# Store sizes by stage in a masked softmax: a half and two quarters for ten batches, then halves, then whole tiles

## Chip, cores, metric

One core of one Trainium2 chip. The metric is device time in microseconds (us), the median of several executions. The granted clock was 1.0 in every run.

## The reference

For each of 16 batches the softmax runs over the first `lengths[b]` of 256 columns, and the rest is zero:

```python
x: (16, 8, 256, 256) float32;  lengths: 16 integers in [128, 256)
result = zeros_like(x)
for b in range(16):
    m = x[b, :, :, :lengths[b]]
    m = exp(m - max(m, axis=-1))
    result[b, :, :, :lengths[b]] = m / sum(m, axis=-1)
```

A batch is 2.097 MB: 128 partitions x 16 rows x 256 columns. In memory one partition's 16 rows are 16 KB in one piece, for the load as for the store.

## The kernel before

Twelve batch slots lie in on-chip memory. SyncE issues the first four loads and all stores; GpSimd issues the other twelve loads, cut to a width that covers the length. VectorE masks (`min` with a cap), ScalarE takes exp and row sums, VectorE multiplies by the inverse, one half batch at a time.

```python
slots, ahead, half = 12, 4, nt // 2          # nt = 16 rows per partition
parts = [slice(0, half), slice(half, half + half // 2), slice(half + half // 2, nt)]
early = batch - slots
s_st = [sem(f"s_st{b}") for b in range(early)] + [sem("s_st")] * slots
...
load(nc.sync, 0, seq_k)                      # and 1, 2, 3
for b in range(batch):                       # SyncE: the stores
    for k, s in enumerate(parts):
        if k < 2:
            nc.sync.wait_ge(s_out, 2 * b + k + 1)
        nc.sync.dma_start(
            out=out_f[b, :, s, :], in_=xt[:, b % slots, s, :]
        ).then_inc(s_st[b], 16)
nc.sync.wait_ge(s_st[-1], 16 * len(parts) * slots)
...
for n in range(ahead, batch):                # GpSimd: the loads
    if n < slots:
        nc.gpsimd.wait_ge(s_fill, n - ahead + 1)
    else:
        nc.gpsimd.wait_ge(s_st[n - slots], 16 * len(parts))
    pick(length(POOL, n), n, widths + [seq_k])   # one load, width by length
...
# VectorE, per batch: mask(b + 1), then for each half: wait for exp, reciprocal, multiply, s_out + 1
```

The softmax here doesn't subtract the row's maximum and nothing guards it: scores larger than these inputs give would overflow.

Of the kernel before, what the change touches and what calls it, by code (L numbers as in the profile page):

```python
# [21 lines left out]
def kernel(  # L22
# [6 lines left out]
    nc = tc.nc  # L29
    P = nc.NUM_PARTITIONS  # L30

    batch, heads, seq_q, seq_k = x.shape
    rows = heads * seq_q
    assert rows % P == 0
    nt = rows // P
    half = nt // 2
# [4 lines left out]
    slots = min(12, batch)  # L41
# [2 lines left out]
    widths = list(range(160, 248, 8))  # L44
    low = widths[0]

    parts = [slice(0, half), slice(half, half + half // 2), slice(half + half // 2, nt)]
    mid = seq_k // 2

    pool = ctx.enter_context(tc.tile_pool(name="all", bufs=1))  # L50
# [14 lines left out]
    inv_sum = pool.tile([P, batch, nt], F32, name="inv_sum")  # L65
    warm = pool.tile([P, 1], F32, name="warm")

    with tc.tile_critical(no_gpsimd_drain=True):  # L68
        sem = lambda n: ctx.enter_context(nc.semaphore(n))
        s_word = sem("s_word")  # L70
        s_word_p = sem("s_word_p")
        s_ones = sem("s_ones")
# [4 lines left out]
        early = batch - slots  # L77
        s_st = [sem(f"s_st{b}") for b in range(early)] + [sem("s_st")] * slots
# [5 lines left out]
        s_out = sem("s_out")  # L84

        def length(engine, b):

            return nc.values_load(  # L88
                (word_p if engine == POOL else word)[0:1, 2 * b : 2 * b + 1],
                engines=[engine],  # L90
                skip_runtime_bounds_check_because="compared with constants, never an address",
            )
# [9 lines left out]
        for b in range(1, ahead):  # L102
            load(nc.sync, b, seq_k)
        for b in range(batch):
            for k, s in enumerate(parts):
                if k < 2:
                    nc.sync.wait_ge(s_out, 2 * b + k + 1)
                nc.sync.dma_start(
                    out=out_f[b, :, s, :], in_=xt[:, b % slots, s, :]
                ).then_inc(s_st[b], 16)  # L110
        nc.sync.wait_ge(s_st[-1], 16 * len(parts) * slots)



        def pick(v, b, ws):

            if len(ws) == 1:
                load(nc.gpsimd, b, ws[0])
                return
            m = (len(ws) - 1) // 2  # L120
            with nc.gpsimd.If(v <= ws[m]):  # L121
                pick(v, b, ws[: m + 1])
            with nc.gpsimd.Else():  # L123
                pick(v, b, ws[m + 1 :])
# [11 lines left out]
        for n in range(ahead, batch):  # L136
            if n < slots:
                nc.gpsimd.wait_ge(s_fill, n - ahead + 1)
            else:
                nc.gpsimd.wait_ge(s_st[n - slots], 16 * len(parts))  # L140
            pick(length(POOL, n), n, widths + [seq_k])


# [56 lines left out]
        for b in range(batch):  # L200
# [3 lines left out]
            for h in range(2):  # L204
                s = slice(h * half, (h + 1) * half)
# [25 lines left out]
                    if (j + 1) % half == 0:  # L231
                        ins.then_inc(s_exp, 1)


# [1 line left out]
_INS = ['x', 'lengths']  # L236
_OUTS = [((16, 8, 256, 256), 'float32')]
# [25 lines left out]
```

## Time and profile before

| | before |
|---|---|
| time, median of 3 (lowest to highest) | 158.04 us (157.88 to 158.11) |
| profiled span | 155.8 us |
| VectorE, ScalarE busy | 78%, 68% |
| bytes moved, mean rate | 62.11 MB, 399 GB/s |
| last load's data, last store's data | 122.6 us, 153.65 us |

The last row is from the trace's packet records. After the last load the DMA engines do nothing for 31 us but push out stores, and for the last 17 of those no engine but the DMA engines works.

### The profile page before, as it was taken

The page shows a single profiled execution, that of the slowest core. Times are in us where ns is not written, and L with a number is a line of the kernel's source. Part 1 is how long each engine was busy: PE and PEld are TensorE (multiplying, and loading weights), DVE is VectorE, ACT ScalarE, POOL GpSimd, SP SyncE. Part 2 cuts the span into 40 slices and gives each one's busy share as a digit, 9 for nine tenths or more (in the row PEclk, how much of TensorE's full clock was granted, in tenths as well). Part 3 has the DMA queues.
Part 4 walks back from the last instruction along what each step waited for, and adds up shares of the span by engine and source line. Part 5 has one row for each costly group of instructions (what it writes and reads, how often), then busy time and mean ns, then how long its engine had stood idle before and what let it go on. Part 6 is the DMA issues. An engine that isn't in the chain of part 4 may idle for free.

```text
span 155.8 us, 1177 instructions
## 1 busy us (share of the span) xinstructions
PE 0.2 (0%) x1; PEld 0.1 (0%) x1; DVE 120.8 (78%) x99; ACT 105.3 (68%) x514; POOL 25.0 (16%) x27
## 2 busy tenths in 40 slices
PE   0000000000000000000000000000000000000000
PEld 0000000000000000000000000000000000000000
DVE  2566999999999999869995999997968999900000
ACT  3009999997979797929696597978692989200000
POOL 5995045742002002010000000000000000000000
DMA  5999999999999999999999999999999999999991
GB/s 126 421 446 421 437 357 386 411 444 426 378 401 405 414 418 412 419 408 405 422 408 414 407 415 408 407 417 409 422 438 426 409 428 413 424 427 428 425 411 50
DMA packets 11607, 62.11 MB, mean 399 GB/s; under 512 B 1058, under 2 KB 1154, under 8 KB 8786
## 3 DMA queue, kind: packets, MB, share of 16 engines
q1 hardware_dynamic: 7488, 41.95, 65.8%
q0 software_dynamic: 4112, 20.12, 32.1%
q14 instruction: 5, 0.04, 0.1%
q10 hardware_dynamic: 2, 0.00, 0.0%
HBM read 28.51 MB, written 33.55 MB: 398 GB/s over the span
## 4 chain that ended last, share of the span: by engine, by line
DMA 33%; DVE 29%; issue 12%; POOL 6%; another core or an unknown queue 4%; POOLq 2%; SPq 1%; DVEq 0%
DMA xt<-in_x_dram 33%; DVE xt L209 17%; DVE xt L182 10%; POOL xt L133 4%; POOL xt L96 2%; DVE inv_sum L207 1%; DVE cap L167 1%; POOLq L88 1%; POOLq L121 1%; SPq L96 1%; DVEq L195 0%; POOLq L123 0%; DVEq L194 0%; SPq L258 0%
## 5 line engine op out<-in xcount | busy, mean ns | idle before, releaser
L225 ACT ACTIVATE xt<-xt x256 | 102.4, 402 | 26.6 <-DVE xt L182 26.6
L209 DVE TENSOR_TENSOR xt<-xt,inv_sum 128x2048 f32<-128x2048 f32 x32 | 73.3, 2292 | 1.1
L225 ACT ACTIVATION_READ_ACCUMULATOR xt<-xt x256 | 48.0, 187 | 0.0
L182 DVE TENSOR_TENSOR xt<-xt,cap 128x2048 f32<-128x2048 f32 x16 | 36.6, 2287 | 11.5 <-DMA xt<-in_x_dram 11.4
L96 POOL DMA_DIRECT2D xt<-in_x_dram x12 | 12.7, 1056 | 41.6 <-issue 41.5
L133 POOL MEMSET xt<- 128x1536 f32 x8 | 11.0, 1426 | 0.3 <-DVE iota_h L157 0.3
L167 DVE TENSOR_SCALAR cap<-iota_h,len_s 128x256 f32<-128x256 f32 x16 | 8.5, 537 | 0.0
L207 DVE RECIPROCAL inv_sum<-row_sum 128x8 f32<-128x8 f32 x32 | 6.2, 195 | 0.0
L157 DVE TENSOR_SCALAR iota_h<-iota_i 128x256 f32<-128x256 int32 x1 | 0.3, 295 | 2.6 <-POOL iota_i L127 2.6
L218 ACT ACT_TABLE_LOAD x1 | 1.3, 1283 | 1.5 <-SPq L68 1.5
L126 POOL DMA_DIRECT2D word_p<-in_lengths_dram x1 | 0.6, 633 | 1.1 <-SPq L68 1.1
L161 DVE COPY len_s<-len_f 128x16 f32<-128x16 f32 x1 | 0.2, 175 | 0.4 <-PE len_f L146 0.4
L127 POOL IOTA iota_i<- 128x256 int32 x1 | 0.4, 360 | 0.1
L218 ACT ACTIVATE warm<-const-float32-0.0 128x1 f32<-128x1 f32 x1 | 0.2, 203 | 0.0
L130 POOL MEMSET ones<- 1x128 bf16 x1 | 0.2, 194 | 0.0
L146 PE MATMUL len_f<-len_b,ones 1*128 1x16 bf16 x1 | 0.2, 168 | 3.1 <-DVE len_b L159 3.1
L159 DVE CAST len_b<-word 1x16 bf16<-1x16 int32 x1 | 0.2, 155 | 0.0
L247 POOL MEMSET const-float32-0.0<- 128x1 f32 x1 | 0.1, 98 | 0.2 <-issue 0.2
L146 PEld LDWEIGHTS len_f<-len_b,ones 1*128 1x128 bf16 x1 | 0.1, 98 | 3.1 <-POOL ones L130 3.1
L247 POOL MEMSET const-bfloat16-1.0<- 128x1 bf16 x1 | 0.1, 99 | 0.0
L247 POOL MEMSET const-uint8-127<- 128x1 uint8 x1 | 0.1, 99 | 0.0
L247 POOL MEMSET const-float32-1.0<- 128x1 f32 x1 | 0.1, 98 | 0.0
## 6 DMA issues: line engine op xcount, KB each, us to landing
out_dram<-xt SPq DMA_DIRECT2D x16, 1024.0 KB, 22.8
out_dram<-xt SPq DMA_DIRECT2D x32, 512.0 KB, 22.7
xt<-in_x_dram SPq DMA_DIRECT2D x4, 2048.0 KB, 14.4
xt<-in_x_dram POOLq DMA_DIRECT2D x3, 1728.0 KB, 54.0
xt<-in_x_dram POOLq DMA_DIRECT2D x2, 2048.0 KB, 37.6
xt<-in_x_dram POOLq DMA_DIRECT2D x2, 1600.0 KB, 36.3
xt<-in_x_dram POOLq DMA_DIRECT2D x2, 1280.0 KB, 61.5
xt<-in_x_dram POOLq DMA_DIRECT2D x1, 1792.0 KB, 39.9
```

Source lines behind the costliest of these rows:

```text
L88: return nc.values_load((word_p if engine == POOL else word)[0:1, 2 * b : 2 * b + 1], engines=[engine], skip_runtime_bounds_check_because= ...
L96: engine.dma_start(out=xt[:, b % slots, :, :w], in_=x_f[b, :, :, :w]).then_inc(s_ld[b], 16)
L121: with nc.gpsimd.If(v <= ws[m]):
L126: nc.gpsimd.dma_start(out=word64_p, in_=lengths[None, :]).then_inc(s_word_p, 16)
L127: nc.gpsimd.iota(iota_i, pattern=[[1, seq_k]], base=0, channel_multiplier=0).then_inc(s_iota, 1)
L133: nc.gpsimd.memset(xt[:, b, :, low:], 0.0).then_inc(s_fill, 1)
L167: nc.vector.tensor_scalar(out=cap[:, b % 4, :], in0=iota_h, scalar1=len_s[:, b : b + 1], scalar2=-1.0e30, op0=ALU.subtract, op1=ALU.mult,)
L182: return nc.vector.tensor_tensor(out=t[:, :, lo:hi], in0=t[:, :, lo:hi], in1=cap[:, b % 4, None, lo:hi].to_broadcast([P, nt, hi - lo]), op ...
L207: step(nc.vector.reciprocal(out=inv_sum[:, b, s], in_=row_sum[:, b, s]))
L209: ins = nc.vector.tensor_tensor(out=t[:, s, :], in0=t[:, s, :], in1=inv_sum[:, b, s, None].to_broadcast([P, half, seq_k]), op=ALU.mult,)
L218: nc.scalar.activation(out=warm, in_=nc.const_aps.tensor(0.0, (P, 1), F32), func=EXP)
L225: ins = nc.scalar.activation(out=e, in_=e, func=EXP, accum_out=row_sum[:, bass.ds(i, 1), j],)
```

## The change

Its intent: while loads run beside the stores, keep store packets small, so that the loads get their share; once no load is left, make them large, since fewer packets cost less.

```diff
-    parts = [slice(0, half), slice(half, half + half // 2), slice(half + half // 2, nt)]
+    quarter = nt // 4
+    cuts = lambda b: (
+        [0, half, half + quarter, nt]
+        if b < slots - 2
+        else [0, half, nt]
+        if b < slots or b == batch - 1
+        else [0, nt]
+    )
+    def parts(b):
+        return [slice(i, j) for i, j in zip(cuts(b), cuts(b)[1:])]
...
-            for k, s in enumerate(parts):
-                if k < 2:
-                    nc.sync.wait_ge(s_out, 2 * b + k + 1)
+            for s in parts(b):
+                nc.sync.wait_ge(s_out, 2 * b + (s.stop - 1) // half + 1)
...
-        nc.sync.wait_ge(s_st[-1], 16 * len(parts) * slots)
+        nc.sync.wait_ge(s_st[-1], 16 * sum(len(parts(b)) for b in range(early, batch)))
...
-                nc.gpsimd.wait_ge(s_st[n - slots], 16 * len(parts))
+                nc.gpsimd.wait_ge(s_st[n - slots], 16 * len(parts(n - slots)))
```

The diff is cut here: it also moves the line that defines `sem`, which changes nothing on the chip. So batches 0 to 9 stay as they were, 10, 11 and 15 go out in halves (8 KB per partition), 12 to 14 whole (16 KB).

More of the change, by code (lines that the diff above doesn't have):

```diff
@@ L66 @@
     warm = pool.tile([P, 1], F32, name="warm")
+    sem = lambda n: ctx.enter_context(nc.semaphore(n))
     with tc.tile_critical(no_gpsimd_drain=True):
-        sem = lambda n: ctx.enter_context(nc.semaphore(n))
         s_word = sem("s_word")
```

## The prediction

> **What bounds the kernel now.** I read the page first, for what is busy when. The page's second part shows it:
>
> ```profile
> DVE  2566999999999999869995999997968999900000
> ACT  3009999997979797929696597978692989200000
> ...
> DMA  5999999999999999999999999999999999999991
> ```
>
> The DMA row stands at 9 from the second slice to the last but one. VectorE and ScalarE stop five slices (some 19 us) before the end. So the 16 DMA engines bound the kernel, and the end is a drain of stores with nothing else running. The page's chain of waits is no guide here: it stops at VectorE's last multiply (134.10 + 2.29 = 136.4 us), because the trace ties no instruction to the final stores.
>
> Next I cut the span into stages, to see how full the engines are in each (columns: stretch, length, busy time of PE, PEld, DVE, ACT and POOL, clock, DMA share, GB/s):
>
> ```profile
> 45.00:75.00 30.00, 0.00 (x0) 0.00 (x0) 27.51 (x24) 24.28 (x120) 2.85 (x3) 1.00 1.02 413
> 75.00:100.00 25.00, 0.00 (x0) 0.00 (x0) 22.54 (x20) 20.02 (x101) 0.00 (x0) 1.00 1.02 410
> 100.00:123.00 23.00, 0.00 (x0) 0.00 (x0) 19.96 (x17) 17.46 (x87) 0.00 (x0) 1.00 1.02 420
> 123.00:129.30 6.30, 0.00 (x0) 0.00 (x0) 6.23 (x6) 5.72 (x30) 0.00 (x0) 1.00 1.01 421
> 129.30:151.40 22.10, 0.00 (x0) 0.00 (x0) 7.03 (x5) 4.06 (x21) 0.00 (x0) 1.00 1.02 423
> 151.40:154.10 2.70, 0.00 (x0) 0.00 (x0) 0.00 (x0) 0.00 (x0) 0.00 (x0) 1.00 0.36 147
> ```
>
> The share is 1.02, not 1.00: packet records overlap a little, so a packet's recorded length is more than it costs. Only the last 2.7 us are ragged; there the engines finish one after another.
>
> Then one batch of the drain (exactly one period, found by trying edges), from the view of the DMA queues:
>
> ```profile
> DMA packets 432, 2.10 MB, mean 424 GB/s; under 512 B 48, under 2 KB 48, under 8 KB 304
> ...
> q1 hardware_dynamic: 432, 2.10, 101.9%
> ...
> out_dram<-xt SPq DMA_DIRECT2D x1, 1024.0 KB, 17.1
> out_dram<-xt SPq DMA_DIRECT2D x2, 512.0 KB, 16.6
> ```
>
> One batch makes 432 packets: 128 of 8 KB (the half, one per partition), 256 of 4 KB (two quarters), 48 of semaphore updates (3 stores x 16 engines). It takes 4.95 us, and a store lands about 17 us after its issue: that is the backlog in the queue.
>
> **What the Trainium skill says.** All three places are in "DMA: Bandwidth & Descriptors". Section "Where 436 GB/s comes from" gives a ceiling of 435.2 GB/s for the 16 engines. The drain's 424 is 97% of it: the trace agrees, and little is left to gain. Section "Why small descriptors are slow (HBM only)" names a fixed overhead of about 3 cycles per packet, besides descriptor metadata. In the packet records of one engine (the one that ends last but one, followed from packet to packet), 4 KB packets are 159 ns long but start every 155.3 ns (152.326, 152.481, 152.636 us), and 8 KB packets are 309 ns long and start every 305.9 ns (148.275, 148.581, 148.887 us). A straight line through the two pitches gives 150.6 ns per 4 KB, which is 27.2 GB/s per engine or 435 for 16, and 4.7 ns fixed per packet. So the trace shows such an overhead, and gives its size. Section "Queues, rings and completion order" says that each engine takes turns between its queues packet by packet. This explains the change's intent: small store packets beside the loads, large ones when no load is left. No view of this one trace tests it.
>
> **The change part by part.** Stores of batches 0 to 9 keep their sizes, and so do all loads, arithmetic and slots. The third store of these batches gets a wait of its own, on a count that the second store has already waited for: nothing on the path. Loads reuse only the slots of batches 0 to 3, whose three stores and count of 48 are unchanged.
>
> What changes is batches 10 to 15. When do their packets run? Stores of one queue go in order. The last load lands at 123.1 us; batch 9's last quarter lands at 124.3 and batch 10's first half, which is 8 KB in both kernels, at 126.4. Everything that differs therefore runs after the loads, in the pure drain. Up to there I expect the same times, to the noise.
>
> In the drain each engine moves 8 partitions of each store. Per batch and engine:
> - Before: 8 x 305.9 + 16 x 155.3 + 3 semaphore packets. Where one of these lies between two 4 KB packets, their starts are 161 ns apart instead of 155, so it costs about 6 ns. Sum: 2,447 + 2,485 + 18 = 4,950 ns, the 4.95 us measured.
> - Halves (batches 10, 11, 15): eight pairs of 4 KB become eight of 8 KB: 8 x (2 x 155.3 - 305.9) = 38 ns, and one semaphore packet fewer: 44 ns saved.
> - Whole tiles (batches 12, 13, 14): a 16 KB packet should cost 305.9 + 2 x 150.6 = 607 ns by the line. 8 x (305.9 + 310.6 - 607) = 75 ns, and two semaphore packets fewer: 87 ns saved.
>
> Sum: 3 x 44 + 3 x 87 = 393 ns. It is all on the path, since the engines have no gap in the drain. SyncE issues 9 stores fewer (48 to 39), at 0.33 us each when not held up; that lies beside a 17 us backlog and is worth nothing. So 158.04 - 0.39 = 157.65 us.
>
> **The rivals.**
> 1. *Record lengths are the cost.* With mean lengths of 161, 313 (median 309) and, from the 16 KB loads, 611 ns, a half saves 8 x (322 - 311) + 9 = 97 ns and a whole tile 8 x (311 + 322 - 611) + 18 = 194 ns, in all 0.87 us: 157.2. Against it: the share of 1.02, and a cap. After batch 10's first half there are 5.5 batches x 2.097 MB = 11.5 MB left, which take 5.5 x 4.95 = 27.2 us now and 26.5 at 435 GB/s. Not more than 0.7 us can come from packet sizes here.
> 2. *16 KB stores are no better than two of 8 KB.* The 16 KB loads at the start are 611 ns long, and the second and third land 4.89 and 4.91 us after the one before, which is a pitch of 611, not 607. Whether that belongs to loads or to 16 KB is open. For stores it would make the whole tiles save 8 x (616.5 - 611) + 12 = 56 ns and the sum 0.30 us: 157.74.
> 3. *Larger stores start too late.* A whole tile has to wait for the second half's multiply. For batch 14 that ends at 129.22 + 2.29 = 131.5 us; the queue gets to it when batch 13 has landed, at 144.2: 12.7 us to spare. For batch 12 it is 115.1 against 134.3. In the changed kernel the drain is at most some tenths earlier, so no gap can open. If I misread it and the queue ran dry before one tile, one half's multiply, 2.4 us with its reciprocal, would be lost: 160.
> 4. *The issuer is held up.* One store issue took 5.7 us (the longest in the trace), some others 1 to 3: SyncE waits when about ten stores are outstanding. A limit in stores would be relieved by fewer, larger ones; a limit in bytes would stay. Neither matters while the backlog is 17 us.
> 5. *The ragged end.* The last two engines finish at 153.57 and 153.65, the others between 152.0 and 152.84. A lag from earlier stages stays as it is when all engines have the same packets to move; larger last packets could move the end by a few hundredths.
>
> **Range and chances.** I take the middle of the first sum, 157.65. The runs of before spread over 0.23 us (157.88 to 158.11), about half of the gain itself, so I give 157.3 to 158.0. A gain of 2% would be 3.2 us, over four times the cap of 0.7 us: 1%. A loss of 2% needs a dry queue or a loss of pace with 16 KB stores that the loads don't show: 1%.
>
> **What would show it.** In the queue view: 1,296 packets fewer on queue 1 (3 x 144 + 3 x 288, so 6,192), and issues of 16 x 1024, 20 x 512 and 3 x 2048 KB. Loads landing at the same times to some tenths, the last near 123. In a drain stretch of whole tiles 431 GB/s (2.097 MB in 4.863 us), of halves 427, of before 424. The span 0.3 to 0.5 us shorter. I am wrong if the GB/s of the whole-tile stretch stays at 424 or falls, if a gap shows in the DMA row after 126 us, or if the times before 123 us move by more than the drain.

## More of the kernel before

One more view of this kernel, which the prediction did not use and should have: the DMA queues between 60 and 90 us (queue, kind: packets, MB, share of 16 engines). Queue 1 holds SyncE's stores, queue 0 GpSimd's loads.

```profile
q1 hardware_dynamic: 1389, 6.63, 54.3%
q0 software_dynamic: 1389, 5.73, 47.7%
```

The packet counts are equal to the last one. This suggests that, while both queues are full, each gets every other packet, and that the sizes of the packets decide how the bandwidth is shared. Experiments 5 and 6 test it.

## The result

| | before | after |
|---|---|---|
| time, median of 6 (lowest to highest) | 157.96 us (157.84 to 158.11) | 157.68 us (157.54 to 157.99) |
| ratio, 95% interval | | 0.9986 (0.9973 to 0.9998) |

Ratios here are the mean time of one kernel's runs over that of the other's of the same rounds, so not quite the ratio of the medians. The means are 0.23 us apart, 0.14%: a little faster in the interval.

The profile after, the page's busy tenths and packets:

```profile
DVE  2567999999999998949995999997977999910000
ACT  3009999997979695957978397979592989400000
...
DMA  4999999999999999999999999999999999999990
...
DMA packets 10311, 62.11 MB, mean 399 GB/s; under 512 B 914, under 2 KB 1010, under 8 KB 7106
...
q1 hardware_dynamic: 6192, 41.95, 65.4%
```

1,296 packets fewer, all on queue 1, as counted in advance. The DMA row has no gap.

The stages of the drain, same columns as in the prediction:

```profile
100.00:123.00 23.00, 0.00 (x0) 0.00 (x0) 20.08 (x19) 17.57 (x87) 0.00 (x0) 1.00 1.02 420
123.00:129.30 6.30, 0.00 (x0) 0.00 (x0) 6.26 (x4) 5.71 (x29) 0.00 (x0) 1.00 1.01 428
129.30:151.40 22.10, 0.00 (x0) 0.00 (x0) 7.60 (x7) 4.67 (x24) 0.00 (x0) 1.00 1.01 429
151.40:154.10 2.70, 0.00 (x0) 0.00 (x0) 0.00 (x0) 0.00 (x0) 0.00 (x0) 1.00 0.17 70
```

Before 123 us the rate is the same, 420. In the drain it is 429 instead of 423, and in the last, ragged stretch the engines are busy 17% of the time instead of 36%: most of them end earlier.

Two whole tiles of that drain (134.5 to 144.22 us), in the view of the DMA queues:

```profile
DMA packets 288, 4.19 MB, mean 432 GB/s; under 512 B 32, under 2 KB 32, under 8 KB 32
...
q1 hardware_dynamic: 288, 4.19, 100.8%
```

256 packets of 16 KB and 32 semaphore updates take 9.72 us, so 4.86 us per tile. Before, a batch took 4.95. The edges of this stretch were chosen to hold exactly two tiles. A stretch with other edges, also of whole tiles alone, reads less:

```profile
134.50:147.00 12.50, 0.00 (x0) 0.00 (x0) 2.47 (x3) 0.00 (x0) 0.00 (x0) 1.00 1.00 427
```

The view counts a packet where it starts, and sixteen packets of 16 KB more or fewer are 21 GB/s in 12.5 us. So the rate of a short stretch can't settle the matter. The distance from one packet's start to the next does: in the packet records, followed on all 16 engines between 134.5 and 148.3 us, it is 607 ns in the mean of 272 steps (607.1).

Where then is the rest of the gain? In the packet records, each engine's last semaphore update tells when that engine was done:

| profile | mean end of the 16 engines | last engine | lag |
|---|---|---|---|
| before | 152.52 us | 153.65 | 1.13 |
| before, second profile | 152.57 | 153.98 | 1.41 |
| after | 151.92 | 153.62 | 1.70 |
| after, second profile | 151.99 | 153.36 | 1.36 |

The mean end moved by some 0.6 us, but the kernel waits for the last engine, and in the first pair of profiles that one moved by 0.03 us. (The second profiles are from the experiments below.)

### The profile page after: what moved, and what is told of

Same layout as the page of the kernel before. It is cut to its first block, busy times and chain, and to the rows that moved or that the text cites. A ratio compares the mean times of both kernels' runs of the same rounds, so it can differ in the third digit from the quotient of the medians.

```text
span 155.7 us, 1168 instructions
## 1 busy us (share of the span) xinstructions
PE 0.2 (0%) x1; PEld 0.1 (0%) x1; DVE 121.3 (78%) x99; ACT 105.2 (68%) x514; POOL 25.1 (16%) x27
## 4 chain that ended last, share of the span: by engine, by line
DVE 33%; DMA 30%; issue 12%; POOL 6%; another core or an unknown queue 4%; POOLq 1%; SPq 1%; DVEq 0%
DMA xt<-in_x_dram 30%; DVE xt L221 18%; DVE xt L194 12%; POOL xt L145 4%; POOL xt L108 2%; DVE inv_sum L219 1%; DVE cap L179 1%; POOLq L100 1%; SPq L108 1%; POOLq L133 0%; DVEq L207 0%; POOLq L135 0%; DVEq L206 0%; SPq L269 0%
## 5 line engine op out<-in xcount | busy, mean ns | idle before, releaser
L179 DVE TENSOR_SCALAR cap<-iota_h,len_s 128x256 f32<-128x256 f32 x16 | 9.1, 572 | 0.0
```

The source lines that it names most:

```text
L179: nc.vector.tensor_scalar(out=cap[:, b % 4, :], in0=iota_h, scalar1=len_s[:, b : b + 1], scalar2=-1.0e30, op0=ALU.subtract, op1=ALU.mult,)
```

## The experiments

Twelve runs were made, and all gave the right result. Each was timed against the kernel before on the same chip.

### 1. The changed kernel and the kernel before, once more

No edit. The first is the measure of noise and a second profile of the change:

> The changed kernel once more, as the measure of noise and for a second profile. Theory (packet pitch): 0.39 us less than before in the drain and nothing before it, so a ratio of 0.9975, with the profile's drain identical to the first one's packet for packet: 16 KB stores every 607 ns, 8 KB every 306. Rival (the gain is only the 0.2 us that the six runs showed, because the stage with loads got slower by some tenths): ratio 0.9985 and the last load again near 123.7 instead of 123.1 us.

Measured: 157.75 us, ratio 0.9991 (0.9970 to 1.0012). The 16 KB packets again start every 607 ns and the 8 KB ones every 306; the last load's data ended at 122.8 us. The second:

> The kernel before, against itself: what ratio and interval come from no change at all, and a second profile of it. Theory (the end is set by the one or two DMA engines that lag behind the others, and that lag arises by chance beside the loads): ratio within 0.001 of 1, the mean end of the 16 engines near 152.5 us as in the first profile, the last engine 0.8 to 1.7 us after the mean. Rival (the lag is fixed): the last engine again 1.13 us after the mean.

Measured: 158.24 us, ratio 1.0006 (0.9991 to 1.0021) for no change at all. The mean end hardly moved (152.57 us), but the lag was 1.41 us this time, not 1.13, so the rival (a fixed lag) falls. This one set is off by 0.1 us, its interval spans 0.5 us, and so the two ratios of the change (0.9986 and 0.9991) cannot tell a gain of 0.2 from one of 0.4. The stage with loads is cleared of suspicion: the last load's data ended at 122.6 and 123.0 us in the two profiles of before, at 123.2 and 122.8 in the two of the change.

### 2. All six last batches whole

```diff
-        else [0, half, nt] if b < slots or b == batch - 1
         else [0, nt]
```

> Batches 10 to 15 all as whole tiles. Pitch theory: three batches more go from halves to whole, 3 x 44 = 0.13 us less than the changed kernel, 0.52 us less than before (ratio 0.9967). Rival (a large last store makes the end ragged, or starts late): same or slower than the changed kernel, with the last engines finishing further apart.

Measured: 157.51 us, ratio 0.9970 (0.9952 to 0.9988). The kernel was sent a second time in the last call:

> The fastest kernel so far once more (batches 10 to 15 whole, no extra wait): pitch theory 0.52 us less than before, ratio 0.9967. Chance (the first ratio, 0.9970, was luck): nearer 0.999. The last engine again 0.8 to 1.7 us after the mean.

Measured: 157.61 us, ratio 0.9965 (0.9948 to 0.9983). The pitch theory's 0.9967 lies between the two. The lags were 1.35 and 1.90 us. The second is above the 0.8 to 1.7 expected, and the longest of all. Two profiles cannot tell whether larger packets at the very end add to the lag; the time shows no loss. This is the fastest version measured, some 0.5 us under the kernel before, and it needs one rule fewer than the change.

### 3. The cost per packet, magnified: 1 KB packets

```diff
-        else [0, half, nt] if b < slots or b == batch - 1
-        else [0, nt]
+        else list(range(nt + 1))
```

> The suspected cost magnified: batches 10 to 15 in sixteen stores each, so packets of 1 KB. Pitch theory (4.7 ns fixed plus 150.6 ns per 4 KB, and 6 ns per semaphore packet): 128 x 42.35 + 16 x 6 = 5,517 ns per batch against 4,950, so 3.4 us more than before, ratio about 1.021. If record lengths were the cost (9 ns fixed): about 6 us more, 1.038. If the issuer is the limit (about ten stores outstanding, then of 128 KB each): the drain shows gaps, and the loss is larger than either.

Measured: 171.99 us, ratio 1.0889. The third guess was right: the issuer became the limit. Two stretches of this kernel (same columns as above):

```profile
124.00:127.50 3.50, 0.00 (x0) 0.00 (x0) 3.46 (x3) 2.92 (x15) 0.00 (x0) 1.00 1.09 380
135.00:160.00 25.00, 0.00 (x0) 0.00 (x0) 0.70 (x1) 0.00 (x0) 0.00 (x0) 1.00 0.80 265
```

While a backlog lasted, the rate was 380 GB/s. The pitch theory gives the same: 16 engines with 8 KB each in 8 x 42.35 + 6 = 345 ns is 380 GB/s. Then the backlog was gone, and SyncE issued one store each 0.49 us, without a pause (0.45 us to issue, 0.04 to the next): 131 KB in 0.49 us is 267 GB/s, the 265 of the second line. So the whole time of this run says nothing on packets; the first stretch does.

### 4. The same with 2 KB packets

```diff
+        else list(range(0, nt + 1, 2))
```

> Packets of 2 KB in the drain (eight stores per batch for batches 10 to 15), small enough to magnify the cost per packet and large enough that the issuer (0.49 us per store in the run with rows) stays ahead of the 5 us that a batch takes to store. Pitch theory: 64 x 80.0 + 8 x 6 = 5,168 ns per batch against 4,950, so 1.3 us more than before, ratio 1.008, and 406 GB/s in the drain. If record lengths were the cost (9 ns fixed per packet): 64 x 84.3 + 8 x 9 = 5,467 against 5,083, 2.3 us more, ratio 1.015. If the issuer still limits it: gaps in the drain and more than either.

Measured: 159.88 us, ratio 1.0107 (1.0088 to 1.0125), between the two theories. Again the stretches tell more:

```profile
123.00:127.00 4.00, 0.00 (x0) 0.00 (x0) 4.00 (x2) 3.76 (x20) 0.00 (x0) 1.00 1.05 407
130.00:150.00 20.00, 0.00 (x0) 0.00 (x0) 6.81 (x5) 3.84 (x20) 0.00 (x0) 1.00 1.03 392
```

With a backlog 407 GB/s, where pitch gives 406. Later 392: by then a store landed 3 us after its issue instead of 17, and fourteen engines finished within 0.2 us of each other, a sign that they had been waiting for work. SyncE again issued without a pause, one store each 0.69 us from 135 us on. Why an issue took that long, when the median of the kernel before is 0.35 us, is not settled. That the engines themselves keep the predicted pitch when they have work is: between 123.5 and 127 us, 2 KB packets of one engine start 80.0 ns apart, the 80.0 of the expectation.

### 5. Large packets beside the loads: every batch whole

```diff
+    cuts = lambda b: [0, nt]
```

> Every batch one whole store, also beside the loads. If packet overhead were all that matters: 16 x 87 = 1.4 us less than before, ratio 0.991. If the engines take turns packet by packet, 16 KB store packets against load packets of 4.3 to 4.8 KB take about three quarters of the bytes while both queues are full: loads land later, VectorE waits for them, the store backlog at the end is small, and the time is 160 us or more (ratio over 1.012).

Measured: 163.53 us, ratio 1.0334 (1.0312 to 1.0357). Overhead alone would have made it faster. The last load's data came at 141.0 us instead of 122.6, and VectorE waited for loads for 28.6 us in all instead of 11.4. Its last stretches:

```profile
123.00:141.00 18.00, 0.00 (x0) 0.00 (x0) 14.46 (x11) 11.78 (x59) 0.00 (x0) 1.00 0.95 398
141.00:159.70 18.70, 0.00 (x0) 0.00 (x0) 11.91 (x9) 7.70 (x39) 0.00 (x0) 1.00 0.80 338
```

After the last load the DMA engines are idle a fifth of the time: they wait for VectorE and ScalarE, which got their input too late. So the time was as the turns said, 160 us or more, and the turns themselves show. Between 44 and 48 us, with both queues full:

```profile
q1 hardware_dynamic: 75, 1.21, 71.7%
q0 software_dynamic: 72, 0.48, 29.3%
```

Packet for packet, 72% of the bytes are stores, about the three quarters of the expectation. In the next 4 us the store queue was nearly empty, and it was 20 packets of stores to 261 of loads.

### 6. Halves, or quarters, beside the loads

```diff
-        [0, half, half + quarter, nt] if b < slots - 2
+        [0, half, nt] if b < slots - 2            # or: [0, 4, 8, 12, 16]
         else [0, nt]
```

> Batches 0 to 9 in halves (8 KB packets beside the loads), 10 to 15 whole. Against the run with the same drain and the old first ten. Packets alone: 10 x 44 = 0.44 us less, about 157.1 us, ratio 0.994. Turn theory: the stores take a larger share beside the loads, so the last load lands later than 124 us; the end stays DMA-bound as long as a backlog is left then, and the time is 157.1 all the same; if the backlog has run out before the last batches are ready, gaps appear in the drain and it is slower than 157.5.

Measured: 161.28 us, ratio 1.0212 (1.0189 to 1.0234). "Later than 124" held, far more than I thought (138.9 us), and the backlog did run out. The DMA queues of this kernel between 30 and 60 us, and its stretch in the drain:

```profile
q1 hardware_dynamic: 951, 6.89, 55.9%
q0 software_dynamic: 951, 5.54, 45.4%
```

```profile
129.30:151.40 22.10, 0.00 (x0) 0.00 (x0) 18.62 (x14) 12.98 (x64) 0.00 (x0) 1.00 0.77 326
```

Packet for packet again, but with larger store packets 6.89 MB of stores to 5.54 of loads. The kernel before, in the same stretch:

```profile
q0 software_dynamic: 1186, 6.45, 53.4%
q1 hardware_dynamic: 1182, 5.89, 48.2%
```

The turns can be seen in the packet records too. In this kernel one engine starts a store packet of 8 KB at 30.291 us, a load packet of 4.8 KB at 30.601, the next store packet at 30.788, load 31.097, store 31.284, load 31.594, and so on. By 90 us six of GpSimd's loads had landed, where the kernel before had seven. VectorE waited for loads for 25.8 us in all instead of 11.4 (the lines of `--waits`, before and here), stores came out later, and with them the backlog went.

```profile
DVE xt L182 <- DMA xt<-in_x_dram: 11.4, 7, 3.0
```

```profile
DVE xt L191 <- DMA xt<-in_x_dram: 25.8, 13, 4.4
```

> Batches 0 to 9 in four quarters (4 KB packets beside the loads), 10 to 15 whole. Packets alone: 10 x 44 = 0.44 us more than the run with the same drain, about 157.95 us, ratio 1.000. Turn theory: the loads get a larger share, so the last load lands earlier than 121 us and the backlog at that point is larger, which buys nothing at the end: 157.95 as well. Rival (loads that land earlier shorten the whole): below 157.5.

Measured: 158.18 us, ratio 1.0009 (0.9991 to 1.0028). The last load's data came at 111.8 us, eleven us earlier, and it bought nothing: the rival falls. The half and two quarters of the first ten batches are thus near the best place: larger starves the loads, smaller pays for packets.

### 7. Without the lag

The lag hides part of what the change does, so I took it away: all engines start the drain together, at the price of a gap.

```diff
         for b in range(batch):
+            if b == slots - 2:      # all stores up to batch 9 have landed
+                nc.sync.wait_ge(s_st[-1], 16 * 18)
```

> The kernel before, with one wait more: the stores of batch 10 are issued only when all stores up to batch 9 have landed. The queue runs dry once, all 16 engines start the drain together, and the lag between them should be gone. Both theories: about 2 us slower than before (batch 9 lands near 124.3, some 2 us to the first packet, then 6 x 4.95 = 29.7 us), ratio about 1.013, the last engine within 0.3 us of the mean. It is the base for the next two.

> The changed kernel with the same extra wait. Theory (the change is worth its packet pitch, 0.39 us, and the lag of one engine hides part of it by chance): the drain from its first packet to the mean end is 0.39 us shorter than in the run with the same wait and the old stores. Rival (the larger packets are worth only the 0.2 us that the timed runs show): 0.2 us shorter.

> The same wait, batches 10 to 15 all whole. Pitch theory: 6 x 87 = 0.52 us shorter in the drain than with the old stores, 0.13 us shorter than with the changed ones. Rival as before: half of that.

| | time, median | ratio to before | drain, mean over the engines from first packet to end | lag |
|---|---|---|---|---|
| old stores | 160.23 us | 1.0142 | 30.56 us | 0.09 |
| changed stores | 159.80 | 1.0102 | 29.76 | 0.13 |
| all six whole | 159.38 | 1.0079 | 29.49 | 0.11 |

The lag is gone, and the gain is plain in time too: 0.43 and 0.85 us by the medians. In the drain it is 0.80 and 1.07 us, twice what I predicted from the pitch, and near what the rival by record lengths gave (0.87 for the change). Each of these drains is one profile, and some 0.1 us of the difference does not reach the end, because the first packet came 0.1 us later with the new stores (125.2 us, against 125.1). Neither theory for these runs held in the drain. (The gap before the first packet was 1.2 us, not 2.) The drain of the old stores and of the changed ones under the extra wait, one line each:

```profile
125.30:154.00 28.70, 0.00 (x0) 0.00 (x0) 11.03 (x9) 7.54 (x38) 0.00 (x0) 1.00 1.02 411
```

```profile
125.30:154.00 28.70, 0.00 (x0) 0.00 (x0) 11.13 (x9) 7.65 (x38) 0.00 (x0) 1.00 1.01 422
```

With the old stores the engines reach 411 GB/s together and 424 when they are spread over 1.6 us. In the records, 4 KB packets that had lasted 159 ns, nearly all of them, now last anything from 156 to 186 (median 164), 16 KB ones 608 to 651 (median 615) instead of 611. From old stores to all whole, each engine saves 16 packets per batch: (1,067 / 6 - 12) / 16 = 10 ns per packet, against 4.7 in the unchanged order. So it seems that a packet costs more when the engines run in step; one profile of each kernel is thin ground for the size. That the engines get in each other's way is the likely reason; no run here shows it, or where.

## Why the prediction was right

- **The bound and the place.** Right: the DMA row has no gap, 420 GB/s before 123 us in both kernels, and the difference lies in the drain.
- **The pitch.** Right to the nanosecond: 16 KB packets of the changed kernel start 607 ns apart (137.454, 138.067, 138.674, 139.281 us, the first step with a semaphore packet in it), as the line through 4 and 8 KB said. A whole tile took 4.86 us (4,863 ns predicted), two profiles show 429 to 430 GB/s between 130 and 150 us, and 430 is what the sum gives there, with some three quarters of that time whole tiles (431) and the rest halves (427). The test of 431 GB/s in a stretch of whole tiles read 432, or 427, by its edges; the 607 ns on all engines settle it.
- **The sum, 0.39 us.** The mean end of the engines moved by 0.53 to 0.65 us, depending on the pair of profiles; 0.06 to 0.15 of that was there before the drain (0.026 to 0.063 MB more moved by 123 us, at 0.42 MB per us), which leaves 0.47 to 0.50, some 0.1 more than the sum. The timed gains, 0.23 and 0.14 us by the means, are smaller, but no change at all measured 0.10 the other way, and the intervals (0.03 to 0.43, and a loss of 0.19 to a gain of 0.47) hold the 0.39. Predicted 157.65, measured 157.68 and 157.75. That this is so near is partly luck: the sum started from 158.04, the median of three runs, and the six runs of before had 157.96.
- **The ragged end, rival 5.** The weak step, and with it "It is all on the path": the time follows the last engine, not the mean. "A lag from earlier stages stays as it is" holds within one drain, where every engine of the kernel before needs the same 4.95 us per batch. But the lag is not the same in each execution: 1.1 to 1.9 us over the profiles of experiments 1 and 2 and of the two kernels. "A few hundredths" was too small for that term; from one profile to another the end moves by several tenths, as much as the change is worth. The last engine ended 0.03 us earlier in the first pair of profiles, 0.62 in the second.
- **Record lengths, rival 1.** Wrong for this kernel (16 KB packets start 607 ns apart, not 611; the records predicted 0.87 us), and near for engines in step (0.80). Its sum takes 311 ns for 8 KB packets where the text gives 313; halves and wholes are three each, so this drops out of the 0.87.
- **16 KB stores no better, rival 2.** Wrong: 607 ns, not 611.
- **Late start and issuer, rivals 3 and 4.** Neither happened: no gap after 126 us. After the first 22 us, SyncE's longest store issue fell from 5.7 to 0.9 us, with 39 stores instead of 48, which fits a limit in stores; it was worth nothing, as said. The issuer was the limit with stores of 128 KB (experiment 3), and perhaps with 256 KB (experiment 4).
- **Turns between queues.** I wrote that no view of the one trace tests it. The queue view did, with equal packet counts, before the experiments confirmed it, and it is the most useful thing about this kernel: the part of the store sizes that the change left alone is worth 4 to 6 us (157.51 against 161.28 with halves; 163.53 with whole tiles).

Open: why one or two engines lag (it is there with the last loads already: in the kernel before, the last engine ended its loads 1.4 us after the mean), and what paces SyncE's small stores.

## What to carry to other kernels

When two queues are full, count their packets: they take turns, so the size of one's packets sets the other's bandwidth, and large stores beside loads can cost far more than their saved overhead. Once a queue is alone, each packet saved gains a few ns (4.7 here), so work out the sum, and the cap that the bandwidth ceiling leaves, before hoping for more. In a drain the last DMA engine sets the end, and its lag varied here by 0.8 us from profile to profile, which can hide a gain of tenths of a microsecond; compare the mean end of the engines too.

## What the Trainium skill lacked or had wrong

- "DMA: Bandwidth & Descriptors", section "Why small descriptors are slow (HBM only)": it has about 3 cycles per packet. The runs show 4.7 ns per packet with the engines spread in time, and about 10 ns (one profile of each kernel) with all 16 in step; the page doesn't tell the two apart.
- Same page, section "Queues, rings and completion order": turns by packet agree with the trace (1,389 packets to 1,389, and the alternation in experiment 6). What it lacks is the consequence: in the trace one contiguous row of 4, 8 or 16 KB is one packet record and one turn, so going from 5.3 to 8 KB store packets on average beside the loads, with the same drain, moved the last load from 121.9 to 138.9 us.
- Same page, section "Rules for kernel authors": at least 1 MiB per DMA for maximum bandwidth. Beside loads, 1 MiB stores cost 3.8 us more than a half and two quarters (161.28 against 157.51 with the same drain); in the drain alone the rule held, by 0.5 us.
- Same page: its part on trn3 counts cycles per DMA instruction for earlier chips, but no page has how the time to issue a store from SyncE depends on the store. The median store of the changed kernel (512 KB to 2 MB) took 0.33 us to issue; stores of 128 KB in packets of 1 KB were issued one each 0.49 us, which capped that drain at 265 GB/s.
- Same page, section "Latency and other measured facts": it has two of the 16 engines as usually slower, without a size. The lag of the last engine behind the mean was 1.1 to 1.9 us at the end of a store queue that stayed full, and 0.1 us where it had run dry. The traces don't number the engines, so no run here shows whether these are the two.
